# Up projection of a decoder layer: seven products for four pairs in every chunk but the first, and low parts made by DMA

## The chip, the cores and the metric

The kernel runs on one core of a Trainium2 chip. The metric is device time in microseconds (us), the median of several runs. The profile comes from one execution taken by the hardware profiler.

## The reference

One decoder layer on 256 tokens of width 2048 in float32: a normalised input projection, two kinds of attention, an output projection with a residual, and a feed-forward part. The change touches the feed-forward part and the step ahead of it:

```
x = x + rmsnorm(mixed @ w_out, norm_attn_post)
h = rmsnorm(x, norm_mlp_pre)                 # (256, 2048)
u = square(relu(h @ w_up))                   # w_up   (2048, 8192)
x = x + rmsnorm(u @ w_down, norm_mlp_post)   # w_down (8192, 2048)
```

## The kernel before, in words

**Matmuls in three passes.** Each float32 operand is split into two fp32r parts: `hi` is a copy rounded to fp32r (ScalarE, ACT) and `lo` is the rest, operand minus `hi` (VectorE, DVE). A product is three matmuls: hi by hi, hi by lo, lo by hi. `split` (L306, L307) does this; `split_gain` (L310, L311) multiplies by a per-partition gain on the way, since the rows of `w_up` have to be multiplied by `norm_mlp_pre`, which lies in `gcol`.

**Weights.** `Weights` keeps one plan of all weight tiles in the order in which TensorE (PE) uses them. A planned tile is loaded by SP (`load`, L190, five `raw` buffers) and split into one of eight pairs of `hi`/`lo` buffers. `get(i)` emits the loads and splits up to tile `i + 1 + ahead` (ahead is 6), as long as no more than eight tiles are unfreed, so tile `i` can be split when tile `i - 8` has been freed. Functions in `first` run when the plan reaches an entry, ahead of it. All engines work off their instructions in the order in which they were emitted.

**The up projection** goes in eight chunks `j` of 1024 columns of `w_up`. A chunk has 16 tiles `k` of 128 rows. A plain step `k` takes 12 matmuls of 128x128 by 128x512: two token blocks `b` times two halves `n` times three passes. Two neighbouring tiles can be taken together as a *pair* `kp` by seven products of 2x2 blocks instead of eight: 7 x 3 = 21 matmuls for what takes 24 as two plain steps. For this, `seven` loads both tiles (1 MB into `ab` or `ab2`), DVE forms sums `t`, `u` of their quarters (L361 to L366), and four tiles are split: the 512 wide `b11`, then `b`, `u`, `t`. On the left side `left_sums` forms sums of blocks of `hT` once, and multiplies by the gain while it does so. In the end `close` adds the shared sums to the four results. `UP_STEPS` gives the order: chunk 0 has no pairs, chunks 1 and 7 have three, chunks 2 to 6 four. In a chunk of four the order is the tiles 8, 9, 10, 11, pair 0, tile 12, pair 1, tile 13, pair 2, tile 14, pair 3, tile 15. "Tile 13" below is the plain tile of rows 13 of a chunk. The left sums of pairs 0 to 2 are made in chunk 0, those of pair 3 in chunk 1.

**Around it.** `residual` (one chain for each token block) normalises the output projection, adds it to `xs`, transposes `xs` on PE (`ht`) and splits the transposes, four channels `k` at a time, into `hT`; these instructions are interleaved with the first steps of chunk 0 by the estimated times of `Flow`. `up_evac` takes relu of an accumulator, transposes it on PE (`rt`), squares it and writes it to `uT[j]` (16 groups of 512 columns; for j 10 to 13 these lie in `ab` and `ab2`, so the last two chunks load some of their pairs as two `raw` tiles). In the down projection `split_u` splits one `uT` group ahead of its use, and the low parts are stored to HBM by SP (`ukeep`) and brought back by POOL.

Of the kernel before, what the change touches and what calls it, by code (L numbers as in the profile page):

```python
# [95 lines left out]
SUMS_AHEAD = 2  # L96


UP_PAIRS = [()] + [("ab", "ab2", "ab", "ab2")] * 5 + [("ab2", "ab", "raw", "ab"), ("ab", "raw", "raw")]


def up_steps(first, *groups):
# [3 lines left out]
    return steps  # L106


THREE = up_steps(range(6, 11), (11, 12), (13,), (14, 15))
FOUR = up_steps(range(8, 12), (12,), (13,), (14,), (15,))  # L110
UP_STEPS = [up_steps(range(16)), THREE] + [FOUR] * 5 + [THREE]

ST = 13 * 256
N_SEVEN = [sum(w == "w" for w, _ in steps) for steps in UP_STEPS]


DOWN_SEVEN = ((7, 11, 13, 17, 19, 23, 25, 29), range(3, 28, 2))
# [51 lines left out]
class Weights:  # L169


    def __init__(self, nc, pool, split, bufs, ahead):
        self.nc, self.pool, self.split_fn = nc, pool, split
        self.bufs, self.limit, self.ahead = bufs, bufs, ahead
        self.specs, self.tiles, self.done = [], [], []
        self.first, self.after = {}, {}

    def plan(self, *spec):

# [13 lines left out]
    def emit(self, upto):  # L193
        upto = min(upto, self.done.index(False) + self.limit, len(self.specs))
        while len(self.tiles) < upto:
            i = len(self.tiles)
            spec = self.specs[i]
            make = len(spec) == 1
            for f in self.first.pop(i, ()):
                f()  # L200
            if not make:
                src, nk, n, g = (*spec, None)[:4]
                w = nk * n
                raw = self.load(src if len(src.shape) == 3 else src.rearrange("(k p) n -> p k n", p=P), w, f"raw{i}")
                for f in self.after.pop(i, ()):
                    f()
            hi = self.pool.tile([P, CW], F32R, tag="hi", bufs=self.bufs, name=f"hi{i}")
            lo = self.pool.tile([P, CW], F32R, tag="lo", bufs=self.bufs, name=f"lo{i}")
            if make:
                spec[0](hi, lo)  # L210
                self.tiles.append((hi, lo))
                continue

            def v(t):
                return t[:, :w].rearrange("p (k n) -> p k n", k=nk)

            cuts = [(o, min(o + 512, w)) for o in range(0, w, 512)] if i < FINE else [(0, w)]
# [46 lines left out]
def layer(nc, tc, io):  # L264
# [49 lines left out]
    def tok(t, k, b):  # L314
        return t[:, k, b * P:(b + 1) * P]
# [25 lines left out]
    def up_weight(j, k):  # L341
        return io["w_up"][k * P:(k + 1) * P, j * CW:(j + 1) * CW]
# [33 lines left out]

    def seven_up(j, kp):
        def load():
            if UP_PAIRS[j][kp] == "raw":
                return [weights.load(up_weight(j, 2 * kp + i), CW, f"raw_w{j}_{kp}{i}") for i in range(2)]  # L380
            return load_two(late[UP_PAIRS[j][kp]], nc.gpsimd if (j, kp) > (1, 0) else nc.sync,
                            io["w_up"][2 * kp * P:(2 * kp + 2) * P, j * CW:(j + 1) * CW])

        return seven(load, lambda: [late["up"].tile([P, CW], F32, tag="T", bufs=2, name=f"{n}{j}_{kp}") for n in "tu"])

# [17 lines left out]
        st, left[c, kp] = down_parts(c, kp)  # L403
        nc.gpsimd.dma_start(out=st.bitcast(F32), in_=skeep[kp])

    def plan_seven(fetch_sums, fs, after, more=(), late_sums=0, last=()):

        at = max(len(weights.specs) - SUMS_AHEAD, after)
        fetch, sums = fetch_sums
        for n, f in (*more, (0, fetch), (-late_sums, sums), *((0, f) for f in last)):  # L410
# [6 lines left out]
    for j in range(FF // CW):  # L417
        wide_u.append([])
        for what, k in UP_STEPS[j]:
            if what == "k":  # L420

                ts = [weights.plan(up_weight(j, k), 1, CW, *([gcol[:, 8 + k:9 + k]] if j < 2 or k >= 2 * max(N_SEVEN) else []))]
            else:
                ts, after = plan_seven(*seven_up(j, k), after, (), SUMS_AHEAD + 1 if not k and N_SEVEN[j - 1] else 0)
            wide_u[j].append((what, k, ts))

    def down_weight(c, k):
# [432 lines left out]
    def residual(b):  # L860

        po, yg, hT = late["po"], late["yg"], late["hT"]
        nc.vector.reduce_sum(ssr[b][:, 0:1], ssy[b], axis=mybir.AxisListType.X)
        r = rstd_of(ssr[b][:, 0:1], 1, D, f"post{b}", (pws[:, 0, b:b + 1], pws[:, 1, b:b + 1]))

        def update(ns):
            cs = [slice(n * 512, (n + 1) * 512) for n in ns]
            for c in cs:
                nc.vector.scalar_tensor_tensor(out=xs[b][:, c], in0=yg[b][:, c], scalar=r, in1=xs[b][:, c],
                                               op0=OP.mult, op1=OP.add)  # L870
# [62 lines left out]
    def up_evac(j, b, i, acc, order):  # L933
# [6 lines left out]
        for k in range(4):  # L940
            transpose(t[:, k * P:(k + 1) * P], r[:, k * P:(k + 1) * P])
        if j not in uT:
            if j in (0, 1, 10, 11, 12, 13):
                t2 = late["u01" if j < 2 else "ab2" if j < 12 else "ab"][:, j % 2 * CW:(j % 2 + 1) * CW]
            else:
                tag = {"tag": "T", "bufs": 2} if j > 13 else {}
                t2 = late["up"].tile([P, CW], F32, name=f"uT{j}", **tag)
# [35 lines left out]
    def left_sums(kp):  # L983
# [6 lines left out]
        for i in range(2):  # L990
            nc.vector.tensor_scalar_mul(f[:, i * S:(i + 1) * S], f[:, i * S:(i + 1) * S], gcol[:, 8 + k + i:9 + k + i])
        fs, qs = [x.rearrange("p (k s) -> p k s", s=P) for x in (f, q)]
        keep = kp >= min(N_SEVEN[1:])
        n = 512 if keep else 384
        tt(out=qs[:, 0], in0=fs[:, 0], in1=fs[:, 1], op=OP.subtract)
        tt(out=qs[:, 3] if keep else fs[:, 1], in0=fs[:, 1], in1=fs[:, 3], op=OP.subtract)
        tt(out=qs[:, 1], in0=qs[:, 0], in1=fs[:, 3], op=OP.add)
        tt(out=qs[:, 2], in0=fs[:, 2], in1=qs[:, 1], op=OP.subtract)
        st = [late["st"][:, 768 * kp + i * n:768 * kp + (i + 1) * n] for i in range(2)]
        yield 3.0  # L1000
        for t, x in ((hs, f), (st, q[:, :n])):
            nc.scalar.activation(t[0], x, AF.Copy)
        yield 1.5
        for t, x in ((hs, f), (st, q[:, :n])):
# [46 lines left out]
    for j in range(FF // CW):  # L1051
# [9 lines left out]
        for t, b in order:  # L1061
# [247 lines left out]
```

## Time and profile before

| | |
|---|---|
| median of 3 runs | 1047.41 us (1047.2 to 1049.08) |
| profiled execution, from its first to its last instruction (span) | 1045.7 us |
| lies around the span, as the median less the span | 1.7 us |
| busy: PE, DVE, ACT, POOL | 99%, 80%, 60%, 5% of the span |
| HBM read, written | 212.72 MB, 15.73 MB |
| output projection's end to up projection's end | 354 to 702 us of the span |

A line of the timeline gives the start in us from the span's start, the duration in us, the engine, the line of the kernel, the operation, its output and inputs, their shapes, and in brackets the idle time of the engine ahead of it with what ended it. PE is TensorE's matmuls, PEld its weight loads. `q` behind an engine marks the DMAs that it issues. Matmuls overlap, so the row of one is longer than the time from one start to the next.

### The profile page before, as it was taken

Reading aid. Unit: us, or ns where it says so; the run is one execution under the profiler, and the core shown is the slowest. Engines: PE = TensorE matmul, PEld = TensorE weight load, DVE = VectorE, ACT = ScalarE, POOL = GpSimd, SP = SyncE. Lnnn points to the kernel's source line nnn. Section 1 sums busy time; section 2 is a strip of 40 time slices with the busy share of each in tenths; the row PEclk is TensorE's granted clock in tenths of the full one; section 3 lists DMA queues with packets and bytes.
Section 4 is the critical chain, followed back from the end, with each engine's and each line's share of the span. In section 5 each row is a group of like instructions: output and inputs, shape, how many; then the busy total and the mean of one; then the engine's idle time right before and its main releaser. Section 6 shows DMA issues by size and latency. Waiting matters only on the chain.

```text
span 1045.7 us, 13378 instructions
## 1 busy us (share of the span) xinstructions
PE 1035.7 (99%) x4837; PEld 863.2 (83%) x4837; DVE 838.7 (80%) x1122; ACT 630.4 (60%) x848; POOL 51.5 (5%) x83
## 2 busy tenths in 40 slices
PE   9999999999999999999999999999999999999996
PEld 6888889888888888888888888888888888888885
DVE  6676536567557669999999999897899978999995
ACT  6674436565545566665765667666567564766661
POOL 0000000000000000000000000000000000111100
PEclk9999999999999999999999999999999999999998
DMA  9975547454447295646657356378778767698952
GB/s 303 370 229 148 140 129 241 146 162 153 150 156 236 92 360 188 216 147 207 202 185 246 121 201 207 113 253 325 274 276 303 265 232 261 238 332 323 356 204 83
DMA packets 79938, 229.33 MB, mean 219 GB/s; under 512 B 6912, under 2 KB 11520, under 8 KB 79488
## 3 DMA queue, kind: packets, MB, share of 16 engines
q1 hardware_dynamic: 64576, 171.47, 48.9%
q0 software_dynamic: 14864, 56.63, 15.2%
q8 instruction: 38, 0.62, 0.3%
q10 hardware_dynamic: 432, 0.37, 0.1%
q14 instruction: 28, 0.23, 0.1%
HBM read 212.72 MB, written 15.73 MB: 218 GB/s over the span
## 4 chain that ended last, share of the span: by engine, by line
PE 97%; DVE 1%; issue 1%; ACT 0%; POOL 0%; DVEq 0%; POOLq 0%; ACTq 0%
PE y L296 25%; PE acc_u L296 24%; PE acc_o L296 8%; PE m L296 7%; PE md L296 5%; PE acc_qk L296 4%; PE acc_v L296 4%; PE acc_ckv L296 2%; PE acc_ukv L296 2%; PE acc_q L296 2%; PE acc_cq L296 2%; PE acc_k L296 2%; PE acc_uq L296 2%; PE rt L300 1%; PE sc_b L296 1%
## 5 line engine op out<-in xcount | busy, mean ns | idle before, releaser
L307 DVE TENSOR_TENSOR lo<-raw,hi 128x1024 fp32r<-128x1024 f32 (+3 forms) x213 | 241.5, 1152 | 89.8 <-ACT hi L306 89.1
L306 ACT ACTIVATE hi<-raw 128x1024 fp32r<-128x1024 f32 (+3 forms) x213 | 209.9, 999 | 73.6 <-PE y L296 16.1
L296 PE MATMUL y<-hi,uhi 128*128 128x512 f32 x370 | 144.4, 390 | 0.0
L296 PE MATMUL y<-hi,ulo 128*128 128x512 f32 x370 | 144.1, 389 | 0.0
L296 PE MATMUL y<-lo,uhi 128*128 128x512 f32 x370 | 144.0, 389 | 0.0
L296 PE MATMUL acc_u<-hi,hT_hi 128*128 128x512 f32 x356 | 141.7, 398 | 0.0
L296 PE MATMUL acc_u<-hi,hT_lo 128*128 128x512 f32 x356 | 139.2, 391 | 0.4 <-DVE hT_lo L307 0.4
L296 PE MATMUL acc_u<-lo,hT_hi 128*128 128x512 f32 x356 | 138.9, 390 | 0.0
L311 DVE SCALAR_TENSOR_TENSOR lo<-raw,gcol,hi 128x1024 fp32r<-128x1024 f32 x74 | 92.5, 1279 | 9.5 <-ACT hi L310 9.5
L310 ACT ACTIVATE hi<-raw,gcol 128x1024 fp32r<-128x1024 f32 x74 | 83.7, 1148 | 25.0 <-DMA raw<-in_w_up 11.7
L296 PEld LDWEIGHTS y<-hi,ulo 128*128 128x128 f32 x370 | 69.5, 188 | 14.4
L296 PEld LDWEIGHTS y<-lo,uhi 128*128 128x128 f32 x370 | 69.5, 188 | 14.3
L296 PEld LDWEIGHTS y<-hi,uhi 128*128 128x128 f32 x370 | 69.5, 188 | 14.2
L296 PEld LDWEIGHTS acc_u<-hi,hT_lo 128*128 128x128 f32 x356 | 66.8, 188 | 14.9 <-DVE hT_lo L307 0.8
L296 PEld LDWEIGHTS acc_u<-lo,hT_hi 128*128 128x128 f32 x356 | 67.0, 188 | 12.8
L296 PEld LDWEIGHTS acc_u<-hi,hT_hi 128*128 128x128 f32 x356 | 67.0, 188 | 12.8
L306 ACT ACTIVATE hi<-u 128x1024 fp32r<-128x1024 f32 (+1 forms) x38 | 37.4, 990 | 49.2 <-DVE u L366 35.4
L307 DVE TENSOR_TENSOR lo<-st_down,hi 128x1024 fp32r<-128x1024 f32 x42 | 50.4, 1220 | 3.0 <-ACT hi L306 2.8
L296 PE MATMUL acc_o<-hi,mixT_hi 128*128 128x512 f32 x128 | 51.8, 405 | 0.0
L306 ACT ACTIVATE hi<-st_down 128x1024 fp32r<-128x1024 f32 x42 | 43.9, 1052 | 12.6 <-PE y L296 9.5
L296 PE MATMUL acc_o<-hi,mixT_lo 128*128 128x512 f32 x128 | 50.2, 392 | 0.0
L296 PE MATMUL acc_o<-lo,mixT_hi 128*128 128x512 f32 x128 | 50.0, 391 | 0.0
(328 smaller groups left out, 2087.7 us busy)
## 6 DMA issues: line engine op xcount, KB each, us to landing
raw<-in_w_down SPq DMA_DIRECT2D x86, 512.0 KB, 5.8
raw<-in_w_up SPq DMA_DIRECT2D x76, 512.0 KB, 4.6
raw<-in_w_in SPq DMA_DIRECT2D x55, 512.0 KB, 4.9
ab<-in_w_up POOLq DMA_DIRECT2D x22, 1024.0 KB, 5.4
raw<-in_w_out SPq DMA_DIRECT2D x32, 512.0 KB, 4.2
ab_down<-in_w_down POOLq DMA_DIRECT2D x11, 1024.0 KB, 7.1
ukeep<-ulo SPq DMA_DIRECT2D x15, 512.0 KB, 7.0
ulo<-ukeep POOLq DMA_DIRECT2D x15, 512.0 KB, 6.2
```

Of the source, the lines that this page charges most:

```text
L296: nc.tensor.matmul(out, a, b, start=start, stop=stop)
L300: nc.tensor.transpose(out, a, ident)
L306: nc.scalar.activation(hi, src, AF.Copy)
L307: nc.vector.tensor_tensor(out=lo, in0=src, in1=hi.bitcast(F32), op=OP.subtract)
L310: nc.scalar.activation(hi, src, AF.Copy, scale=g)
L311: nc.vector.scalar_tensor_tensor(out=lo, in0=src, scalar=g, in1=hi.bitcast(F32), op0=OP.mult, op1=OP.subtract)
```

## The change

- Chunks 1 and 7 get a fourth pair, so every chunk but the first has four pairs and the order of the old chunks of four.
- For tiles 11, 13 and 15 of chunk 0, and 9, 10, 11, 13 and 14 of every other chunk (38 in all), `lo` is no longer made on DVE: ACT copies the weight to `hi`, ACT copies `hi` times -1 to `lo`, and a POOL DMA adds the weight from HBM to `lo`.
- The gain of tiles 8 to 15 moves from the weights into `hT`: in `residual` their splits are made one channel at a time, with a gain. Weight tiles keep a gain only in chunk 0, tiles 0 to 7.
- All pairs are loaded by SP into `ab` and `ab2` in turn, and the load stands four plan entries ahead of where it stood.
- The left sums of pair 3 follow those of pair 2 in chunk 0, and they too rewrite `hT`.
- `uT` 2 to 7 are stored to HBM by SP after their squares (`u_away`); groups 10 to 13 take the places of 4 to 7. Groups 2 and 3 come back in chunk 7, and 4 to 7 at the start of the down projection into `ab` and `ab2` (`u_back`).

```
-UP_PAIRS = [()] + [("ab", "ab2", "ab", "ab2")] * 5 + [("ab2", "ab", "raw", "ab"), ("ab", "raw", "raw")]
+N_SEVEN = [0] + [4] * 7
+K_SCALED = 8
+BY_DMA = {0: (11, 13, 15), **{j: (9, 10, 11, 13, 14) for j in range(1, 8)}}
...
-UP_STEPS = [up_steps(range(16)), THREE] + [FOUR] * 5 + [THREE]
+UP_STEPS = {0: up_steps(range(16)), 4: up_steps(range(8, 12), (12,), (13,), (14,), (15,)),
...
+UP_STEPS = [UP_STEPS[n] for n in N_SEVEN]
+PAIR_AHEAD = 4
...
+            if i in self.by_dma:
+                self.nc.scalar.activation(hi[:, :w], raw[:, :w], AF.Copy)
+                self.nc.scalar.activation(lo[:, :w], hi[:, :w].bitcast(F32), AF.Copy, scale=-1.0)
+                self.nc.gpsimd.dma_start(out=lo[:, :w], in_=src, accum_op=OP.add)
...
     def seven_up(j, kp):
         def load():
-            if UP_PAIRS[j][kp] == "raw":
-                return [weights.load(up_weight(j, 2 * kp + i), CW, f"raw_w{j}_{kp}{i}") for i in range(2)]
-            return load_two(late[UP_PAIRS[j][kp]], nc.gpsimd if (j, kp) > (1, 0) else nc.sync,
-                            io["w_up"][2 * kp * P:(2 * kp + 2) * P, j * CW:(j + 1) * CW])
+            buf = late[("ab", "ab2")[(sum(N_SEVEN[:j]) + kp) % 2]]
+            return load_two(buf, nc.sync, io["w_up"][2 * kp * P:(2 * kp + 2) * P, j * CW:(j + 1) * CW])
...
-                ts = [weights.plan(up_weight(j, k), 1, CW, *([gcol[:, 8 + k:9 + k]] if j < 2 or k >= 2 * max(N_SEVEN) else []))]
+                ts = [weights.plan(up_weight(j, k), 1, CW, *([gcol[:, 8 + k:9 + k]] if not j and k < K_SCALED else []))]
+                if k in BY_DMA[j]:
+                    weights.by_dma.add(ts[0])
...
-            split(hT[0][:, 4 * n:4 * n + 4, b * P:(b + 1) * P], hT[1][:, 4 * n:4 * n + 4, b * P:(b + 1) * P], tv)
+            for k in [range(4 * n, 4 * n + 4)] if 4 * n < K_SCALED else [range(k, k + 1) for k in range(4 * n, 4 * n + 4)]:
+                split(*[tok(x[:, k[0]:k[-1] + 1], slice(None), b) for x in hT], tv[:, k[0] - 4 * n:k[-1] + 1 - 4 * n],
+                      gcol[:, 8 + k[0]:9 + k[0]] if len(k) == 1 else None)
...
+        if b and 2 <= j < 8:
+            flow.start(u_away(j), 6.0)
+
+    U_HOME = {2: 8, 3: 9, 10: 4, 11: 5, 12: 6, 13: 7}
+    uaway = {}
+
+    def u_away(j):
+        uaway[j] = dram.tile([P, CW], F32, name=f"uaway{j}")
+        nc.sync.dma_start(out=uaway[j], in_=uT.pop(j).rearrange("p k s -> p (k s)"))
+        yield 0
+
+    def u_back(j, t):
+        nc.sync.dma_start(out=t, in_=uaway[j])
+        uT[j] = t.rearrange("p (k s) -> p k s", k=4)
...
-        yield from left_sums(2)
+        for kp in range(2, 4):
+            yield from left_sums(kp)
...
-            if (j, what, k, b) == (1, "k", 8, 0):
-                fourth = flow.start(left_sums(3), 20.0)
-            if j == 2 and t == 0:
-                flow.finish(fourth)
+            if (j, t, b) == (FF // CW - 1, 6, 0):
+                for i in (2, 3):
+                    u_back(i, late["up"].tile([P, CW], F32, tag=f"k{i}", bufs=1, name=f"uT{i}_back"))
...
+    for i in range(4, 8):
+        u_back(i, late["ab" if i < 6 else "ab2"][:, i % 2 * CW:(i % 2 + 1) * CW])
```

More of the change, by code (lines that the diff above doesn't have):

```diff
@@ L106, in up_steps @@
     return steps
-THREE = up_steps(range(6, 11), (11, 12), (13,), (14, 15))
-FOUR = up_steps(range(8, 12), (12,), (13,), (14,), (15,))
-UP_STEPS = [up_steps(range(16)), THREE] + [FOUR] * 5 + [THREE]
-ST = 13 * 256
-N_SEVEN = [sum(w == "w" for w, _ in steps) for steps in UP_STEPS]
+UP_STEPS = {0: up_steps(range(16)), 4: up_steps(range(8, 12), (12,), (13,), (14,), (15,)),
+            5: up_steps(range(10, 14), (), (14,), (), (), (15,))}
+UP_STEPS = [UP_STEPS[n] for n in N_SEVEN]
+PAIR_AHEAD = 4
+ST = 12 * 256
 DOWN_SEVEN = ((7, 11, 13, 17, 19, 23, 25, 29), range(3, 28, 2))
@@ L175, in __init__ @@
         self.specs, self.tiles, self.done = [], [], []
-        self.first, self.after = {}, {}
+        self.first, self.after, self.by_dma = {}, {}, set()
     def plan(self, *spec):
@@ L404, in down_back, with plan_seven @@
         nc.gpsimd.dma_start(out=st.bitcast(F32), in_=skeep[kp])
-    def plan_seven(fetch_sums, fs, after, more=(), late_sums=0, last=()):
+    def plan_seven(fetch_sums, fs, after, more=(), late_sums=0, last=(), ahead=0):
         at = max(len(weights.specs) - SUMS_AHEAD, after)
         fetch, sums = fetch_sums
-        for n, f in (*more, (0, fetch), (-late_sums, sums), *((0, f) for f in last)):
+        for n, f in (*more, (ahead, fetch), (-late_sums, sums), *((0, f) for f in last)):
             weights.first.setdefault(at - n, []).append(f)
@@ L420, in layer @@
             if what == "k":
-                ts = [weights.plan(up_weight(j, k), 1, CW, *([gcol[:, 8 + k:9 + k]] if j < 2 or k >= 2 * max(N_SEVEN) else []))]
-            else:
-                ts, after = plan_seven(*seven_up(j, k), after, (), SUMS_AHEAD + 1 if not k and N_SEVEN[j - 1] else 0)
+                ts = [weights.plan(up_weight(j, k), 1, CW, *([gcol[:, 8 + k:9 + k]] if not j and k < K_SCALED else []))]
+                if k in BY_DMA[j]:
+                    weights.by_dma.add(ts[0])
+            else:
+                ts, after = plan_seven(*seven_up(j, k), after, (), SUMS_AHEAD + 1 if not k and N_SEVEN[j - 1] else 0,
+                                       ahead=PAIR_AHEAD)
             wide_u[j].append((what, k, ts))
@@ L989, in left_sums @@
         tt(out=f, in0=hs[0].bitcast(F32), in1=hs[1].bitcast(F32), op=OP.add)
-        for i in range(2):
-            nc.vector.tensor_scalar_mul(f[:, i * S:(i + 1) * S], f[:, i * S:(i + 1) * S], gcol[:, 8 + k + i:9 + k + i])
         fs, qs = [x.rearrange("p (k s) -> p k s", s=P) for x in (f, q)]
-        keep = kp >= min(N_SEVEN[1:])
+        keep = k >= K_SCALED
         n = 512 if keep else 384
+        if not keep:
+            for i in range(2):
+                nc.vector.tensor_scalar_mul(f[:, i * S:(i + 1) * S], f[:, i * S:(i + 1) * S], gcol[:, 8 + k + i:9 + k + i])
         tt(out=qs[:, 0], in0=fs[:, 0], in1=fs[:, 1], op=OP.subtract)
@@ L998, in left_sums @@
         tt(out=qs[:, 2], in0=fs[:, 2], in1=qs[:, 1], op=OP.subtract)
-        st = [late["st"][:, 768 * kp + i * n:768 * kp + (i + 1) * n] for i in range(2)]
+        home = late["st4"] if keep else late["st"][:, 768 * kp:768 * kp + 768]
+        st = [home[:, i * n:(i + 1) * n] for i in range(2)]
+        split_of = ((st, q[:, :n]),) if keep else ((hs, f), (st, q[:, :n]))
         yield 3.0
-        for t, x in ((hs, f), (st, q[:, :n])):
+        for t, x in split_of:
             nc.scalar.activation(t[0], x, AF.Copy)
         yield 1.5
-        for t, x in ((hs, f), (st, q[:, :n])):
+        for t, x in split_of:
             tt(out=t[1], in0=x, in1=t[0].bitcast(F32), op=OP.subtract)
```

11 lines of the change are left out of this document (7 added, 4 removed).

## The prediction

> **What bounds the kernel now.** I read the page first, then the order of TensorE's instructions, then the stages.
>
> ```profile
> span 1045.7 us, 13378 instructions
> PE 1035.7 (99%) x4837; PEld 863.2 (83%) x4837; DVE 838.7 (80%) x1122; ACT 630.4 (60%) x848; POOL 51.5 (5%) x83
> PEclk9999999999999999999999999999999999999998
> PE 97%; DVE 1%; issue 1%; ACT 0%; POOL 0%; DVEq 0%; POOLq 0%; ACTq 0%
> ```
>
> TensorE (PE) is busy for 99% of the span at a full granted clock, and 97% of the chain that ended last is its own work. A busy matmul can still hide a gap, because the rows overlap: one row lasts 0.39 us while the next starts earlier. So I took the starts in order of time. One pair by seven products, of chunk 3:
>
> ```profile
> 500.14 0.39 PE L296 MATMUL m<-hi,hT_hi 128*128 128x512 f32 x1
> ...
> 504.69 0.39 PE L296 MATMUL m<-hi,hT_lo 128*128 128x512 f32 x1
> 504.92 0.39 PE L296 MATMUL acc_u<-hi,hT_hi 128*128 128x512 f32 x1
> ```
>
> From the first to the last line lie the pair's 21 matmuls; the next step starts at 504.92. (504.92 - 500.14) / 21 = 0.2276 us from start to start. That is the price of one matmul, not the 0.39 us of the row. Then the stages, by windows (busy us and count of PE, PEld, DVE, ACT, POOL; clock; DMA share; GB/s):
>
> ```profile
> 365.00:403.00 38.00, 37.59 (x172) 30.87 (x171) 29.50 (x45) 23.51 (x32) 2.39 (x3) 1.00 0.81 305
> 534.80:577.50 42.70, 42.70 (x197) 35.37 (x196) 41.01 (x45) 28.08 (x33) 2.85 (x4) 1.00 0.61 198
> 706.00:760.00 54.00, 54.00 (x248) 44.73 (x247) 43.06 (x49) 31.98 (x37) 1.43 (x2) 1.00 0.81 296
> ```
>
> The second row is one chunk with four pairs. VectorE (DVE) works 41.01 of 42.70 us, yet PE has no gap. So relieving DVE gives nothing by itself: only fewer matmuls shorten this stage, and whatever makes PE wait lengthens it. The one place in the up projection where PE loses time is its start, below.
>
> **The matmuls removed.** Chunks 1 and 7 go from three pairs by seven to four. A pair by seven is 21 matmuls where two plain steps are 24, so 2 x 3 = 6 matmuls go: 6 x 0.2276 = 1.37 us, all on the path. No other matmul or transpose goes.
>
> **The splits in `residual`.** For channels 8 to 15 each split of four channels at once becomes four splits with a gain. For token block 0 these stand on DVE just ahead of block 1's normalisation:
>
> ```profile
> 357.71 0.68 DVE L307 TENSOR_TENSOR hT_lo<-ht,hT_hi 128x512 fp32r<-128x512 f32 x1
> ...
> 359.50 0.68 DVE L307 TENSOR_TENSOR hT_lo<-ht,hT_hi 128x512 fp32r<-128x512 f32 x1
> 360.10 1.28 DVE L311 SCALAR_TENSOR_TENSOR lo<-raw,gcol,hi 128x1024 fp32r<-128x1024 f32 x1
> 361.30 0.15 DVE L863 TENSOR_REDUCE ssr<-ssy 128x1 f32<-128x4 f32 x1
> 361.48 0.27 DVE L500 TENSOR_SCALAR t_post<-ssr,pws 128x1 f32<-128x1 f32 x1
> 362.43 0.75 DVE L869 SCALAR_TENSOR_TENSOR x<-yg,rstd_post,x 128x512 f32<-128x512 f32 x1 [0.67 <-POOL rstd_post L501]
> 363.01 0.39 PE L296 MATMUL acc_u<-hi,hT_lo 128*128 128x512 f32 x1
> 363.32 0.63 PE L300 MATMUL ht<-ident,x 128*128 128x128 f32 x4
> 366.67 0.50 PE L296 MATMUL acc_u<-hi,hT_lo 128*128 128x512 f32 x1 [0.41 <-DVE hT_lo L307]
> ```
>
> DVE has no gap up to the reduction at 361.30, which feeds POOL's power and the update at 362.43; the update is done at 363.18 and the transposes that read it start at 363.32, 0.31 us after the matmul ahead of them instead of 0.23. PE waits there already by 0.08 us, so a delay on DVE passes through. A 512-wide split holds DVE 360.10 - 359.50 = 0.60 us. The nearest rows to the new ones are these, 128 wide:
>
> ```profile
> 386.72 0.28 DVE L995 TENSOR_TENSOR c<-c 128x128 f32<-128x128 f32 x1
> 387.04 0.29 DVE L996 TENSOR_TENSOR c<-c 128x128 f32<-128x128 f32 x1
> 387.25 0.29 DVE L997 TENSOR_TENSOR c<-c 128x128 f32<-128x128 f32 x1
> 387.57 0.29 DVE L998 TENSOR_TENSOR c<-c 128x128 f32<-128x128 f32 x1
> ```
>
> They start 0.21 to 0.32 us apart. Four take 0.84 to 1.28 us, 0.24 to 0.68 more than one wide split; two groups, 0.5 to 1.4 us. I take the middle, 0.265 each: 2 x (1.06 - 0.60) = 0.92 us, all of it PE's, since the wait is there already. The lower end for this step is a small gain: if the wait of 0.41 us at 366.67 closes through another order, -0.4.
>
> The Trainium skill (Perfetto Trace Analysis, Optimizing Scalar/DVE Operations) speaks against this step: it gives DVE a fixed cost of about 125 ns for each instruction on PSUM and advises grouping. By that figure three more instructions in each of two groups would cost an estimated 0.75 us, which the rows above bracket.
>
> **38 low parts by DMAs.** Off DVE, onto ScalarE (ACT): a copy to hi, a copy of -hi to lo, then a POOL DMA that adds the weight to lo. In a chunk DVE loses five instructions like this one, and ACT gains five like the second:
>
> ```profile
> 550.43 1.28 DVE L311 SCALAR_TENSOR_TENSOR lo<-raw,gcol,hi 128x1024 fp32r<-128x1024 f32 x1
> 545.24 1.05 ACT L306 ACTIVATE hi<-t 128x1024 fp32r<-128x1024 f32 x1
> 546.19 1.15 ACT L310 ACTIVATE hi<-raw,gcol 128x1024 fp32r<-128x1024 f32 x1
> 552.63 1.15 ACT L310 ACTIVATE hi<-raw,gcol 128x1024 fp32r<-128x1024 f32 x1
> 555.33 0.39 PE L296 MATMUL acc_u<-lo,hT_hi 128*128 128x512 f32 x1
> 562.81 0.39 PE L296 MATMUL acc_u<-lo,hT_hi 128*128 128x512 f32 x1
> 545.95 0.71 POOL L374 DMA_DIRECT2D ab<-in_w_up  x1 [8.65 <-DVE lo L307]
> ```
>
> DVE falls by 5 x 1.28 to about 34.6 us of a chunk, ACT rises from 28.08 by 5 x 1.05 to about 33.3: neither becomes a bound. What counts is the distance from ACT to PE. Tile 13's hi starts on ACT at 546.19 (the block before it runs back to back, 545.24 + 0.95); its -hi would end at 546.19 + 0.95 + 1.05 = 548.19; PE's first use of its lo is at 555.33. The DMA has 7.14 us from issue to landing. Tile 14: 552.63 + 2.00 = 554.63 to 562.81, 8.18 us. The others have more: a tile can start when the one eight places back is free, so PE has the seven tiles between; for 9 and 10 these are 57 matmuls (13.0 us), for 11 66 (15.0 us), in chunk 0 84 (19.1 us), less 2.0 us for ACT.
>
> No accumulating DMA is in this trace. The nearest rows (KB each, median us from issue to landing):
>
> ```profile
> raw<-in_w_up SPq DMA_DIRECT2D x76, 512.0 KB, 4.6
> ab<-in_w_up POOLq DMA_DIRECT2D x22, 1024.0 KB, 5.4
> ab_down<-in_w_down POOLq DMA_DIRECT2D x11, 1024.0 KB, 7.1
> ukeep<-ulo SPq DMA_DIRECT2D x15, 512.0 KB, 7.0
> ulo<-ukeep POOLq DMA_DIRECT2D x15, 512.0 KB, 6.2
> u<-in_w_down POOLq DMA_DIRECT2D x6, 1024.0 KB, 8.4
> c<-in_w_down POOLq DMA_DIRECT2D x4, 1024.0 KB, 8.9
> ```
>
> It writes 512 KB and must read both the weight and what is in lo, so I bound it by 4.6 us (512 KB, quiet) and 8.9 us (1024 KB, busy). The stage gets busier: 198 GB/s x 42.7 us = 8.5 MB in a chunk now, plus five tiles (2.6 MB) and, in three chunks, two stored tiles (1.0 MB) is 11 to 12 MB, 260 to 285 GB/s, near the down projection's 296. I take 6.2 us, the 512 KB POOL load under that traffic: it lands 0.9 us ahead of tile 13's use. Cost 0, and the cover is thin.
>
> **Moved at no cost.** The pair loads go from POOL to SP, four plan entries earlier; an SP load of a pair waits until its buffer is read, and the weight loads behind it wait too. Released at 545.95 (now POOL's row), it holds tile 14's weight behind it, which ACT wants at 552.63: 6.7 us, more than the 4.6 of a weight load. POOL's accumulating DMAs wait for ACT, and behind them stand only further ones. The six stores wait on SP for the squares; the down projection runs such stores on SP (ukeep, x15) with PE busy 54.00 of 54.00 us. The tiles that come back at the start of the down projection are split one group ahead of their use, after three groups of 48 matmuls (32.8 us) at the earliest. The fourth pair's left sums move into chunk 0, where DVE works 29.50 of 38.00 us. Dropped gains save about 0.1 us on tiles that are not waited for.
>
> **Sum.** Against the profiled span: 1045.7 - 1.37 + 0.92 = 1045.25 us. The median of the runs, 1047.41, stands 1.7 us above the span; with the same difference, 1046.96, rounded to 1046.9. A difference under 0.2% (2.1 us) is about what a measurement of this kernel can't tell from no change, so this is no change.
>
> **Rivals.**
> - *The accumulating DMA lands too late* (slower). It decides at 7.14 us from issue to landing; from 8.18 on tile 14 adds to it. At 8.4 us, the 1024 KB row: 7 chunks x (1.26 + 0.22) = 10.4 us, 1057.3. At 8.9: 7 x (1.76 + 0.72) = 17.4 us, 1064.3. For it: 1 MB is read in all, and the stage comes near the traffic under which 1024 KB took 7.1 to 8.9. Against it: 1024 KB from POOL takes 5.4 in the up projection. Chance 0.30. The Trainium skill (Collectives: The Full Stack, The bandwidth ceiling) says that a reducing DMA reads two sources over one ring and so runs at half a copy's rate; no run here shows it yet, and by that rule the 1024 KB rows are the right ones.
> - *SP's order makes tile 14 late* (slower). If the pair's megabyte ahead of its weight takes the 8.4 us of a busy load, the weight lands no sooner than 545.95 + 8.4 = 554.35, lo's copy ends at 556.35 and the DMA has 6.46 us; at 7.1 us that is 0.64 x 7 = 4.5 us, 1051.4. Chance 0.11.
> - *The delay in `residual` does not reach PE* (lower). Then 1.37 us stay, and with the wait of 0.41 us closed as well 1047.41 - 1.78 = 1045.6, still inside 0.2%. For more than 2.1 us something would have to go that no row of PE shows. Chance of over 0.2% faster: 0.09.
>
> **The numbers.** Forecast with its neighbours inside 0.2%: 0.50; faster 0.09; slower 0.30 + 0.11 = 0.41. The range's low end is 1045.2, 0.4 under the lowest case. Its high end, 1062, takes in the first rival up to a landing of about 8.7 us and leaves out what lies beyond. The forecast's own range, by its bounds (0.5 to 1.4 us in `residual`, -0.4 if the wait closes), is 1045.6 to 1047.5.
>
> **What would show it.** Right: six matmuls fewer; PE's start-to-start time still 0.2276 us; DVE near 35 us in a chunk, ACT near 33; accumulating DMAs landing in under 7.1 us; PE's wait ahead of block 1's transposes near 1 us instead of 0.08. Wrong: idle time of PE put down to POOL's DMA into lo at the 13th or 14th tile of each chunk, a period of a chunk above 42.7 us, or SP waiting on a pair's buffer while ACT waits for a weight.

## The result, and the profile after

The changed kernel takes 1093.01 us (median of 4 runs, 1090.13 to 1096.96), the kernel before 1047.88 us beside it (4 runs, 1047.2 to 1049.08). The ratio is 1.0435, 95% interval 1.0411 to 1.0458: 45 us slower, where I forecast no change and let the range end at 1062.0.

The page of the changed kernel (busy, clock and chain rows as before):

```profile
span 1090.6 us, 13430 instructions
PE 1046.5 (96%) x4831; PEld 865.4 (79%) x4831; DVE 804.3 (74%) x1103; ACT 667.8 (61%) x902; POOL 70.0 (6%) x99
PEclk9999999999999899899999999999999999999999
PE 78%; DMA 9%; issue 5%; DVE 4%; ACT 2%; SPq 0%; POOL 0%; POOLq 0%; DVEq 0%; ACTq 0%
```

Six matmuls are gone (4837 to 4831), DVE is 34 us less busy and ACT 37 us more, as the change intends. But PE's own work, 97% of the chain before, is now 78%; DMAs, DVE and "issue" hold 18%. And there are slices in which the clock is below full. The waits of PE (total us, times, longest):

```profile
PE acc_u L305 <- DMA lo<-in_w_up: 27.9, 13, 3.5
PE ht L309 <- DVE x L879: 5.0, 1, 5.0
PE rt L309 <- ACT r L949: 0.9, 4, 0.2
```

All of it lies in the up projection: from its first matmul to its last it took 347.2 us before and takes 392.1 now, and the 335.8 us behind it are the same. Nearly the whole difference of the two spans, 1090.6 - 1045.7 = 44.9 us, can be laid out from the trace. The three rows give 33.8 us. Around each of the 14 long waits some 0.16 us more is lost (a matmul at 537.44 behind one at 535.91 starts 1.30 us late by the spacing of 0.2276, and its row says 1.14), 2.2 us. The clock record has four stretches at 0.5, of 6.83, 6.83, 3.41 and 3.41 us, 20.5 us in all. In the first two PE was still waiting, for 2.9 and 1.3 us, which the rows have counted; half of the 16.3 us left, 8.1 us, is lost. Less 1.37 us for the six matmuls: 42.7 us. The other 2.2 us are steps of PE that are 0.1 to 0.2 us too long, most of them right behind these waits.

**The residual's wait.** Rows of DVE, ACT, PEld and PE at the splits of block 0:

```profile
357.52 0.35 DVE L320 SCALAR_TENSOR_TENSOR hT_lo<-ht,gcol,hT_hi 128x128 fp32r<-128x128 f32 x1
357.90 0.37 ACT L319 ACTIVATE hT_hi<-ht,gcol 128x128 fp32r<-128x128 f32 x1 [1.73 <-DVE hT_lo L320]
358.30 0.35 DVE L320 SCALAR_TENSOR_TENSOR hT_lo<-ht,gcol,hT_hi 128x128 fp32r<-128x128 f32 x1 [0.43 <-ACT hT_hi L319]
358.68 0.37 ACT L319 ACTIVATE hT_hi<-ht,gcol 128x128 fp32r<-128x128 f32 x1 [0.42 <-DVE hT_lo L320]
359.08 0.35 DVE L320 SCALAR_TENSOR_TENSOR hT_lo<-ht,gcol,hT_hi 128x128 fp32r<-128x128 f32 x1 [0.43 <-ACT hT_hi L319]
358.74 0.19 PEld L305 LDWEIGHTS acc_u<-hi,hT_hi 128*128 128x128 f32 x1
366.70 0.15 DVE L873 TENSOR_REDUCE ssr<-ssy 128x1 f32<-128x4 f32 x1
368.73 1.09 PE L309 MATMUL ht<-ident,x 128*128 128x128 f32 x4 [5.04 <-DVE x L879]
```

A low part has to wait for its own high part. But the next channel's high part waits for the low part before it, whose result it doesn't need. Both use the PSUM tile `ht`. They have `hT_hi` in common, too, one reading and the other writing it; but PEld reads `hT_hi` at 358.74 while ACT writes another channel of it (358.68 to 359.05), and neither waits. That leaves `ht`. So the two engines take turns, and a channel costs 358.30 - 357.52 = 0.78 us. The reduction that starts at 361.30 before starts at 366.70 now.

**Tiles 13 and 14.** The rows that decide in chunk 3, of ACT, POOL, SP and PE:

```profile
528.09 1.06 ACT L221 ACTIVATE lo<-hi 128x1024 fp32r<-128x1024 f32 x1
529.45 0.87 POOL L222 DMA_DIRECT2D lo<-in_w_up  x1 [20.92 <-ACT lo L221]
537.44 0.50 PE L305 MATMUL acc_u<-lo,hT_hi 128*128 128x512 f32 x1 [1.14 <-DMA lo<-in_w_up]
526.50 0.38 SPq L383 DMA_DIRECT2D ab<-in_w_up  x1
526.93 0.47 SPq L971 DMA_DIRECT2D uaway<-uT  x1
527.44 0.43 SPq L192 DMA_DIRECT2D raw<-in_w_up  x1
536.30 1.06 ACT L220 ACTIVATE hi<-raw 128x1024 fp32r<-128x1024 f32 x1 [2.86 <-DMA raw<-in_w_up]
538.74 0.87 POOL L222 DMA_DIRECT2D lo<-in_w_up  x1 [8.42 <-ACT lo L221]
547.95 0.50 PE L305 MATMUL acc_u<-lo,hT_hi 128*128 128x512 f32 x1 [2.74 <-DMA lo<-in_w_up]
```

Tile 13's DMA has from 529.45 to PE's first wish for `lo`, some 1.14 us ahead of 537.44: 6.85 us. It takes 8.0. Tile 14 is late before its DMA is issued: its weight stands on SP behind a pair and a store, was issued at 527.44 and reached ACT at 536.30, 8.9 us later. Then the DMA takes 9.2 us. In the waits of PE by time, tile 14 has 17.3 us of the 27.9, tile 13 has 7.1, and tile 11 of chunk 0, whose high part the residual's splits held up on ACT, 3.4 (0.84 in experiment 1, where the splits are grouped). The median landings of the three kinds of load (KB each, us), and ACT's wait for weights:

```profile
raw<-in_w_up SPq DMA_DIRECT2D x72, 512.0 KB, 8.2
ab<-in_w_up SPq DMA_DIRECT2D x28, 1024.0 KB, 5.7
lo<-in_w_up POOLq DMA_DIRECT2D x38, 512.0 KB, 7.7
ACT hi L220 <- DMA raw<-in_w_up: 20.5, 10, 4.8
```

**The clock.** Windows right behind four waits (the last three columns are clock, DMA share, GB/s), with two of the waits:

```profile
369.50:372.50 3.00, 3.00 (x10) 2.31 (x9) 2.96 (x6) 0.60 (x1) 0.97 (x1) 0.50 0.00 0
450.00:453.00 3.00, 3.00 (x8) 2.31 (x7) 0.00 (x0) 0.00 (x0) 0.00 (x0) 0.50 1.07 369
596.00:599.00 3.00, 3.00 (x15) 2.47 (x14) 0.00 (x0) 0.64 (x1) 0.00 (x0) 1.00 1.05 422
643.00:645.00 2.00, 2.00 (x6) 1.51 (x6) 0.12 (x1) 1.21 (x2) 0.47 (x1) 0.50 1.02 418
595.53 0.50 PE L305 MATMUL acc_u<-lo,hT_hi 128*128 128x512 f32 x1 [2.91 <-DMA lo<-in_w_up]
641.03 0.50 PE L305 MATMUL acc_u<-lo,hT_hi 128*128 128x512 f32 x1 [2.06 <-DMA lo<-in_w_up]
```

PE is "busy" throughout in all four, but in the rows at 0.50 it gets through fewer matmuls. The wait of 2.06 us was followed by half a clock and the longer one of 2.91 us was not; the last section says why.

### The profile page after: what moved, and what is told of

Its sections match the earlier page's. It is cut to its first block, busy times and chain, and to the rows that moved or that the text cites. A ratio compares the mean times of both kernels' runs of the same rounds, so it can differ in the third digit from the quotient of the medians.

```text
span 1090.6 us, 13430 instructions
## 1 busy us (share of the span) xinstructions
PE 1046.5 (96%) x4831; PEld 865.4 (79%) x4831; DVE 804.3 (74%) x1103; ACT 667.8 (61%) x902; POOL 70.0 (6%) x99
## 4 chain that ended last, share of the span: by engine, by line
PE 78%; DMA 9%; issue 5%; DVE 4%; ACT 2%; SPq 0%; POOL 0%; POOLq 0%; DVEq 0%; ACTq 0%
PE y L305 24%; PE acc_u L305 12%; PE acc_o L305 8%; DMA lo<-in_w_up 7%; PE md L305 5%; PE acc_v L305 4%; PE acc_qk L305 4%; PE m L305 3%; PE acc_ckv L305 2%; PE acc_ukv L305 2%; PE acc_q L305 2%; PE acc_cq L305 2%; PE acc_k L305 2%; DMA raw<-in_w_up 2%; PE acc_uq L305 2%
## 5 line engine op out<-in xcount | busy, mean ns | idle before, releaser
L316 DVE TENSOR_TENSOR lo<-raw,hi 128x1024 fp32r<-128x1024 f32 (+3 forms) x237 | 270.5, 1159 | 106.7 <-ACT hi L315 105.4
L315 ACT ACTIVATE hi<-raw 128x1024 fp32r<-128x1024 f32 (+3 forms) x237 | 235.3, 1006 | 86.4 <-DMA raw<-in_w_in 18.5
L305 PE MATMUL acc_u<-lo,hT_hi 128*128 128x512 f32 x344 | 138.4, 402 | 28.1 <-DMA lo<-in_w_up 27.9
L305 PE MATMUL acc_u<-hi,hT_hi 128*128 128x512 f32 x344 | 139.4, 405 | 0.0
L305 PEld LDWEIGHTS acc_u<-hi,hT_lo 128*128 128x128 f32 x344 | 66.1, 192 | 13.8
L220 ACT ACTIVATE hi<-raw 128x1024 fp32r<-128x1024 f32 x38 | 40.0, 1053 | 42.9 <-DMA raw<-in_w_up 20.5
L1074 DVE TENSOR_TENSOR c<-m,c 128x512 f32<-128x512 f32 x28 | 18.7, 689 | 58.5 <-ACT c L1071 57.1
L316 DVE TENSOR_TENSOR lo<-ab,hi 128x512 fp32r<-128x512 f32 (+1 forms) x56 | 52.5, 954 | 11.4 <-ACT hi L315 11.4
L222 POOL DMA_DIRECT2D lo<-in_w_up x38 | 33.3, 878 | 309.6 <-ACT lo L221 269.5
```

The lines of the kernel that those rows point to most:

```text
L220: self.nc.scalar.activation(hi[:, :w], raw[:, :w], AF.Copy)
L222: self.nc.gpsimd.dma_start(out=lo[:, :w], in_=src, accum_op=OP.add)
L305: nc.tensor.matmul(out, a, b, start=start, stop=stop)
L315: nc.scalar.activation(hi, src, AF.Copy)
L316: nc.vector.tensor_tensor(out=lo, in0=src, in1=hi.bitcast(F32), op=OP.subtract)
L1074: tt(out=c[out], in0=x, in1=y, op=op)
```

## Experiments

**1. The residual's splits grouped.** For eight channels: first four high parts on ACT, then four low parts on DVE.

```
-for k in ...: split(one channel, gain)
+for k in ks: nc.scalar.activation(hT_hi[k], tv[k], AF.Copy, scale=gain[k])
+for k in ks: nc.vector.scalar_tensor_tensor(out=hT_lo[k], in0=tv[k], scalar=gain[k], in1=hT_hi[k], ...)
```

> The changed kernel, but in residual the four hi copies of a group come first and then the four lo parts, instead of hi, lo, hi, lo. Theory 1 (two engines that read one PSUM bank are put one after the other, so the eight single splits go back and forth between ACT and DVE at 0.78 us a channel and hold up block 1's normalisation): the 5.04 us wait ahead of block 1's transposes falls under 1.5 us, the half-clock stretch of 6.8 us behind it goes (3.4 us), and ACT reaches chunk 0's tile 11 earlier, so its 3.44 us wait shrinks: 1093 less 8 to 12 is 1081 to 1085. Rival (the small instructions themselves are slow, or block 1 waits for something else): the wait stays over 3 us and the time over 1089. The waits at tiles 13 and 14 of the later chunks stay in both.

1085.37 us (1083.24 to 1086.28), ratio 1.0352 [1.0336, 1.0367]: 7.6 us back, 0.4 less than the least that was expected. DVE's four low parts and PE's two waits:

```profile
358.86 1.12 DVE L898 SCALAR_TENSOR_TENSOR hT_lo<-ht,gcol,hT_hi 128x128 fp32r<-128x128 f32 x4
PE acc_u L305 <- DMA lo<-in_w_up: 24.7, 14, 4.1
PE ht L309 <- DVE x L879: 0.7, 1, 0.7
```

The next instruction on DVE starts at 359.89, so four take 1.03 us, 0.26 each. The wait falls from 5.04 to 0.70 us. Taking turns was the cost, not the number of instructions.

**2. The single splits alone, in the kernel before.**

```
-split(four channels at once)
+for k in ([four] if n < 2 else singles): split(one channel)
```

> The kernel before with one part of the change alone: in residual channels 8 to 15 are split one at a time, hi, lo, hi, lo (without the gain, which stays in the weights). Theory 1: the wait ahead of block 1's transposes grows from 0.08 to about 5 us, and a stretch at half clock follows (3.4 us lost), with at most 1 us more at tile 8 of chunk 0: 1053 to 1057. If the halved clock needs more than this wait, 1052.5 to 1053.5. Rival (the changed kernel's 5 us came from elsewhere): under 1050.

1053.59 us (1052.89 to 1054.11), ratio 1.0051 [1.0036, 1.0066]. The same wait appears without anything else of the change, and behind it 3.41 us at half a clock:

```profile
PE ht L300 <- DVE x L869: 4.6, 1, 4.6
```

**3. No accumulating DMAs**, on the grouped kernel; those 38 low parts are made on DVE again.

```
-BY_DMA = {0: (11, 13, 15), **{j: (9, 10, 11, 13, 14) for j in range(1, 8)}}
+BY_DMA = {j: () for j in range(8)}
```

> As the first, and all low parts on DVE again; four pairs in chunks 1 to 7, pair loads on SP, stores and returns of six groups stay. Theory 1 (the low parts by DMA make PE wait, nothing else in the up projection does): no wait of PE on lo, about 1047.4 - 1.4 + 0.5 = 1046 to 1048.5. Rival 2 (the added traffic and the longer SP queue make everything late): 6 of the 26 MB added and SP's order stay, so waits of a few us remain, over 1051.

1053.12 us (1052.01 to 1053.57), ratio 1.0045 [1.003, 1.006]: 32.3 us less than experiment 1. PE waits for no DMA, and there is no half clock. But the 1046 to 1048.5 expected are missed. The larger part of what is left is new, two waits for the relus at the ends of chunks 1 and 7:

```profile
PE rt L309 <- ACT r L956: 3.7, 2, 2.0
```

**4. A plain load in place of the accumulating one**, on the grouped kernel; `lo` then holds the weight and not the rest.

```
-nc.gpsimd.dma_start(out=lo, in_=src, accum_op=OP.add)
+nc.gpsimd.dma_start(out=lo, in_=src)
```

> As the first, but POOL's DMA into lo is a plain load of the same 512 KB instead of an accumulating one; what PE multiplies in these 38 low parts is then the weight, not its rest. If accumulating itself is what is slow (it reads both sides), landing falls from 7.7 to about 6 us and the waits at tiles 13 and 14 fall from 26 us to under 8: about 1060. If the queue and the traffic around it are what is slow, landing stays over 7 us and the time within 5 us of the first kernel's.

1069.87 us (1069.4 to 1071.68), ratio 1.0212 [1.0195, 1.0229]. This lies between the two times expected. So 15.5 of experiment 3's 32.3 us go with the adding, and 16.8 stay with a plain load:

```profile
lo<-in_w_up POOLq DMA_DIRECT2D x38, 512.0 KB, 5.4
PE acc_u L305 <- DMA lo<-in_w_up: 12.3, 6, 3.1
```

It lands 2.0 us sooner than the accumulating one (7.4 in experiment 1). Five of the six waits are at tile 14, whose weight is still late: ACT waits 12.5 us for such weights in the up projection.

**5. The pairs on POOL**, as before the change, on the grouped kernel.

```
-load_two(buf, nc.sync, ...)
+load_two(buf, nc.gpsimd if (j, kp) > (1, 0) else nc.sync, ...)
```

> As the first, but the pair loads go back to POOL's queue (all but the first), still four plan entries early. If tile 14 is late since its weight stands behind a pair's megabyte on SP (ACT waited 2.86 us for it in chunk 3), ACT's waits on weights in the up projection go and tile 14's wait falls from about 2.8 to under 1 us in each chunk: 1060 to 1072. If only the accumulating DMA's landing counts, the time stays within 4 us of the first kernel's, or gets worse where an accumulating DMA stands behind a pair load on POOL.

1077.34 us (1076.26 to 1079.36), ratio 1.028 [1.0265, 1.0296]. ACT's waits for weights fall from 22.5 to 3.4 us, and PE's on the DMAs from 24.7 to 13.8. But a pair now queues with the accumulating DMAs, and the 1060 to 1072 of the first theory are missed:

```profile
ab<-in_w_up POOLq DMA_DIRECT2D x27, 1024.0 KB, 10.0
PE rt L309 <- ACT r L956: 6.1, 5, 2.1
```

The pairs are late instead of the weights: ACT waits 21.5 us for them. On neither queue did all loads land in time.

**6. Only the tiles between pairs: 13 and 14 of chunks 1 to 7**, on the grouped kernel (`BY_DMA = {0: (), 1..7: (13, 14)}`).

> As those, with low parts by DMA for tiles 13 and 14 alone. Theory 1: nearly all the waits of the first kernel on lo in chunks 1 to 7 come back (about 23 us with the halved clock's share of 7, and the closing sums' waits of up to 4 us return): 1070 to 1084. Rival (9 to 11 load the queues and make 13 and 14 late): waits under half, 1053 to 1065.

1081.35 us (1080.3 to 1081.63), ratio 1.0315 [1.0299, 1.033]; 14 DMAs, landing in 8.5 us, make almost all the wait that 38 make:

```profile
PE acc_u L305 <- DMA lo<-in_w_up: 24.2, 12, 3.6
```

**7. Only the tiles ahead of the pairs: 9, 10 and 11** (`1..7: (9, 10, 11)`).

> Four hi copies first in residual, and low parts by DMA only for tiles 9, 10 and 11 of chunks 1 to 7. Theory 1 (a DMA made low part costs PE only where the tile is needed too soon after its hi; 9 to 11 have 13 to 15 us of PE's work between a free buffer and their use): no wait on lo, and DVE reaches the closing sums 3.8 us earlier than in the kernel without DMAs, so the waits of 1.75 and 1.99 us at the ends of chunks 1 and 7 go: 1046.5 to 1048.5. Rival (every accumulating DMA costs, by its traffic): waits of a few us on 9 to 11, over 1051.

1055.49 us (1054.47 to 1057.31), ratio 1.0072 [1.0057, 1.0087]. PE waits for none of the 21 DMAs, landing in 6.6 us. It misses the 1046.5 to 1048.5 expected, by a wait at all seven ends of chunks: 1.72 us at the end of chunk 1, 0.22 to 0.64 at the next five, 2.08 after chunk 7. Rows of ACT and PE at the end of chunk 1, and the same in the kernel before at the end of chunk 2:

```profile
PE rt L309 <- ACT r L956: 5.7, 7, 2.1
452.19 1.06 ACT L315 ACTIVATE hi<-u 128x1024 fp32r<-128x1024 f32 x1 [3.74 <-DVE u L375]
453.15 0.67 ACT L956 ACTIVATE r<-acc_u,rstd_pre 128x512 f32<-128x512 f32 x1
453.88 0.66 PE L309 MATMUL rt<-ident,r 128*128 128x128 f32 x4 [1.72 <-ACT r L956]
```

```profile
492.55 1.06 ACT L306 ACTIVATE hi<-u 128x1024 fp32r<-128x1024 f32 x1 [3.74 <-DVE u L366]
493.51 0.67 ACT L937 ACTIVATE r<-acc_u,rstd_pre 128x512 f32<-128x512 f32 x1
494.67 0.60 PE L300 MATMUL rt<-ident,r 128*128 128x128 f32 x4
```

The second relu of a chunk stands behind the next pair's copy `hi<-u`, for which ACT idles 3.74 us until DVE has formed `u`. That order is not new: the kernel before has it too, with the same 3.74 us, and its relu starts 1.16 us ahead of PE's transposes, without a wait. What is new is the time left. DVE's closing sums start 7.3 us ahead of these transposes in the kernel before (487.40), and here 5.1 us ahead of PE's wish for them (447.03 to 452.16). Why they start later is not shown.

**8. Tile 12 as well** (`1..7: (9, 10, 11, 12)`).

> As the kernel with tiles 9, 10, 11, with tile 12 too. Tile 12 stands between pairs as 13 does, but has 57 matmuls (13.0 us) between a free buffer and its use, where 13 and 14 have 45 (10.2 us). Theory 1 (distance decides): no wait or under 0.5 us a chunk, 1046.5 to 1050. Rival (any tile between two pairs is late, since its weight stands behind a pair's megabyte on SP): waits of 1 to 3 us a chunk, 1055 to 1070.

1061.26 us (1059.9 to 1063.33), ratio 1.0132 [1.0115, 1.0148], 5.8 us for seven DMAs more. Four of tile 12's seven uses wait, 4.7 us in all (2.02, 1.29, 1.17, 0.21). So tile 12 is late even with 57 matmuls to its use, by less than tile 14. The time is in the rival's range, but the rival's reason isn't in the rows. In the four chunks with a wait, the copies of tile 12 wait for no weight; they stand behind the chunk's relus on ACT:

```profile
546.13 1.09 ACT L220 ACTIVATE hi<-raw 128x1024 fp32r<-128x1024 f32 x1
548.61 0.87 POOL L222 DMA_DIRECT2D lo<-in_w_up  x1 [14.95 <-ACT lo L221]
```

PE wants this `lo` at 553.96, 5.35 us after the issue, and the median landing is 6.4.

**9. The pairs and nothing else.** No DMA adds; the gain of tiles 8 to 15 stays in the weights; the residual's split is four wide as before.

```
+BY_DMA = {j: () for j in range(8)}
-weights.plan(..., gain if not j and k < K_SCALED else [])
+weights.plan(..., gain if not j or k >= K_SCALED else [])
+split(four channels at once)
```

> The changed kernel without low parts by DMA and without the gain in residual (the gain of tiles 8 to 15 stays in the weights, four channels are split at once as before): what is left is the fourth pair in chunks 1 and 7, the pair loads on SP, and the six groups in HBM. Theory 1: no wait of PE on any DMA; six matmuls less (1.37 us) against the waits for relu at the ends of chunks 1 and 7 that came with the full DVE (1.75 and 1.99 us): 1047.9 to 1050.5. Rival (SP's order and the 6 MB more cost by themselves): PE waits on weights, over 1052.

1053.49 us (1052.37 to 1054.87), ratio 1.0056 [1.0044, 1.0069]. Not a gain, and in the rival's range. PE loses 1.8 us at the end of chunk 1, at the same place as in experiment 7, and 2.2 at the end of chunk 7:

```profile
PE rt L309 <- ACT r L947: 4.2, 3, 2.2
696.97 2.12 SPq L973 DMA_DIRECT2D ab<-uaway  x4
707.57 1.06 ACT L315 ACTIVATE hi<-raw 128x1024 fp32r<-128x1024 f32 x1 [5.61 <-DMA raw<-in_w_down]
```

After chunk 7 there is no next pair. There two copies of the down projection's weights stand ahead of the relu, and the first waits 5.61 us for its weight; in the kernel before such a wait is 1.9 us at most. SP has just issued the returns of four groups, 2 MB, and the next three of these weights stand behind them (from 699.18). That is the rival's cause, by the order of the rows; the returns were not tried elsewhere.

**10. The same with less lookahead in the last pair of a chunk** (`weights.ahead -= 3` instead of 1).

> As that kernel, but in the last pair of a chunk the plan runs three entries less ahead instead of one, so fewer splits of plain tiles stand ahead of the closing sums on DVE. Theory 1 (the waits for relu come from the five splits ahead of the closing sums): the waits of 1.75 and 1.99 us go, 1046.3 to 1047.5, the six matmuls' worth below the kernel before. Rival (with three entries ahead the next chunk's first tiles come late): waits on lo at tiles 8 and 9, over 1050.

1066.79 us (1064.85 to 1068.93), ratio 1.0183 [1.0169, 1.0197]. A miss, with a time in the rival's range: tiles were held back so long that one came late itself, not 8 or 9 but tile 12, by 0.97 us in each of five chunks and 2.08 in chunk 7, with 3.67 us more for the relu after it and 3.41 us at half a clock behind each of the last two. It says nothing for or against the place.

```profile
PE acc_u L305 <- DVE lo L320: 6.9, 6, 2.1
```

**11 and 12. The relus earlier in ACT's program, their transposes later in PE's**, in the kernels of 9 and of 7.

```
-up_evac(2 * j + n, b, at[b, n], accs[b, n], o + 0.6)
+up_evac(2 * j + n, b, at[b, n], accs[b, n], 0.5 * (o + 0.6), lag)   # lag ahead of the transposes
```

> This is the pairs without any DMA (no accumulating DMAs, the residual split four wide as before), with the relus of a chunk's four accumulators put earlier in ScalarE's program and their transposes later in TensorE's. Without the reordering that kernel took 1053.49 us; TensorE waited 4.2 us for `r` (1.8 at the end of chunk 1, 2.2 at the end of chunk 7), and there ScalarE's second relu stood behind the copy `hi<-u` of the next pair, for which it idled 3.74 us. Theory: this place in ScalarE's program is the whole loss beside the pairs' six matmuls, so the wait on `r` goes and the time is 1048.5 to 1050, with the fast end 1047.7 - 1.37 = 1046.3 if nothing else comes late. Rival: VectorE is simply full with four pairs and no DMA (847 us busy), the next tile or sum is late instead, and it stays over 1052.

> The accumulating DMAs only for tiles 9, 10 and 11 of chunks 1 to 7, residual grouped, and the same reordering of relus and transposes. Without the reordering this took 1055.49 us, with 5.7 us of TensorE's waits on `r` in seven chunks and none on an accumulating DMA. Theory: the seven waits are all the one place in ScalarE's program; they go, and the time is 1048.5 to 1050.5 (residual wait 0.7 us left). Rival: ScalarE, with 42 copies more, delays something else by as much, and it stays over 1053.

1055.84 us (1054.53 to 1057.57), ratio 1.0077 [1.0063, 1.0091], and 1055.12 us (1052.97 to 1057.08), ratio 1.0072 [1.0059, 1.0084]. Both expectations are missed, and both times lie in the rival's range. The waits at the ends of chunks 1 to 6 go in both, though the edit moves relus and transposes at once, so it doesn't tell which of the two was needed. The wait after chunk 7 stays, longer than before (2.36 and 3.36 us), with 3.41 us at half a clock behind it. In experiment 12 ACT's row there is

```profile
710.50 1.06 ACT L315 ACTIVATE hi<-raw 128x1024 fp32r<-128x1024 f32 x1 [6.04 <-DMA raw<-in_w_down]
```

with a second such copy after it: after chunk 7 the relus stand behind the down projection's weights. In experiment 11 DVE's closing sums are now late by 0.23 us in most chunks, as its rival had it.

**13 and 14. The same place mended after chunk 7 as well:** there the lookahead is raised again 3 us later, so that one copy instead of two stands ahead of the relus. Number 13 has the DMAs for tiles 9, 10 and 11; number 14 has none, and early relus in chunks 1 and 7 only.

```
-weights.ahead = W_AHEAD
+flow.start(ahead_again(), 3.0)      # sets weights.ahead = W_AHEAD
```

> The kernel with accumulating DMAs for tiles 9, 10 and 11 and early relus (1055.12 us; TensorE waited 3.36 us for `r` at 711, after chunk 7, and its clock was halved for 3.41 us behind it), with one more edit, at the end of chunk 7 alone: the four relus come before the next copies, and the lookahead of the weights is raised again 3 us later, so that one copy `hi<-raw` of the down projection and not two stand in ScalarE's program ahead of the relus. Theory: the wait there falls to under 1.2 us (the second copy's wait on its DMA and its time were 2.74 us), the halving goes, and the time is 1050 to 1052. Rival: the wait stays over 2 us, since the first copy waits for a DMA (710.5) as late as before, and the time stays over 1054.

> The pairs without any DMA (1053.49 us; TensorE waits for `r` 1.8 us at the end of chunk 1 and 2.2 us at the end of chunk 7), with the relus early at the ends of chunk 1 and chunk 7 only and the lookahead raised 3 us later after chunk 7. Theory: both waits fall to under 0.5 us and the time is 1048.5 to 1050.5, still not under the kernel before by what a measurement can tell. Rival: over 1052, as the same edit in all chunks gave 1055.84 us.

1051.84 us (1050.59 to 1052.56), ratio 1.0033 [1.0021, 1.0046], and 1050.9 us (1050.39 to 1052.11), ratio 1.0029 [1.0019, 1.004]. In 13 the wait after chunk 7 falls to 0.6 us and the half clock goes, as expected. In 14, 0.4 us above the range expected, both mended waits go, but one of 1.72 us appears at the end of chunk 2, which had none. Of all fourteen, these two come nearest to the kernel before, and both are slower than it.

```profile
PE rt L309 <- ACT r L947: 1.7, 1, 1.7
```

## Why the prediction was wrong, step by step

The medians share out the 45.1 us: the residual's splits 7.6 (the change against experiment 1), the DMAs 32.3 (1 against 3), and 5.2 for what is left, four pairs with DVE making all low parts (3 against the kernel before).

- **The matmuls removed: right.** Six fewer, 0.2276 us each at a full clock. Beside them PE's trace has only the wait of 0.41 us to give back in this stretch, so some 1.8 us was the most there was to gain. No run's total shows it.
- **The splits in `residual`: the term was mis-sized,** 0.92 us against a wait of 5.04. Its price for a DVE instruction was right: 0.265 us was taken, 0.26 measured once they are grouped. What failed is that I counted DVE's instructions by themselves. As `split` emits them, DVE and ACT work on one PSUM tile in turn, at 0.78 us a channel, in two groups of four channels. The Trainium skill (PSUM — Partial Sum Buffer, PSUM bank collisions raise a hardware error) says that accesses of two engines to the same bank have to be kept apart, reads among them, and that a scheduler orders any two such instructions. The rows at 357.52 to 359.08 agree with that, and I weighed another page at this step, on the cost of one instruction. That taking turns is the cost, experiment 1 shows; that the turns come of the PSUM tile in common is what the rows leave, and the instructions were not tried on two banks.
- **38 low parts by DMAs: the rule that I put beside the row was nearer than the row.** I took 6.2 us for landing and allowed 7.14 us; in chunk 3 it took 8.0 and had 6.85. The first rival, 0.30, is what happened. Its price was too low: it took 8.4 us for both tiles, 10.4 us in all, while tile 14 took 9.2 us and was issued late, so the waits came to 27.9. The rule of half a copy's rate, which the Trainium skill (Collectives: The Full Stack, The bandwidth ceiling) gives for the reducing step of a collective, has the right sign here: 7.4 us against 5.4 for a plain load of the same size from the same queue. The ratio is 1.4, not 2, by medians of runs whose other traffic is not the same.
- **Moved at no cost: wrong for the pairs on SP.** The step set 6.7 us against a landing of 4.6 for tile 14's weight. With pairs, stores and weights on one queue the median landing is 8.2, and 8.9 for the tile shown. The queue alone doesn't make it so: in experiment 3, with the same loads on SP and no accumulating DMAs, it is 6.4. This is the second rival, counted as an alternative to the first; they happened together, and each made the other worse. Experiment 4 takes away the adding and experiment 5 the pairs from SP, and in each about half of PE's 24.7 us of waits on these DMAs stays (12.3 and 13.8). The step priced the groups that come back by their own use alone; that SP's weights for the down projection stand behind them (experiment 9) was in no term.
- **The clock was in no term.** I priced a late tile by its wait alone. 8.1 of the 44.9 us are matmuls at half a clock behind waits.
- **DVE and ACT: right as sums; the conclusion is open.** The prediction had them near 35 and 33 us in a chunk. Measured in a chunk of four pairs (DVE the third figure, ACT the fourth):

```profile
577.50:624.70 47.20, 43.15 (x196) 34.77 (x195) 34.66 (x39) 31.70 (x38) 3.98 (x6) 1.00 0.79 246
```

  I wrote that relieving DVE gives nothing by itself. For chunks 2 to 6 that stands. Chunks 1 and 7 with four pairs and DVE making every low part lose about 4 us behind the relus, which the changed kernel, with its DMAs, doesn't (0.9). That this is the relief of DVE is not shown. In experiment 7 DVE makes 21 low parts fewer than in experiment 3, and the wait for the relus is longer, 5.7 us against 3.7. In the changed kernel PE also stands still for 1.4 to 3.5 us at tile 14 of every chunk, shortly ahead of the relus, which gives ACT and DVE the time as well.
- **The range** took in landings up to about 8.7 us and no second cost at the same time. Its sum of rivals was made as if one at most could come true.

What stays open is the last 3 to 4 us of experiments 13 and 14. Each mend moved a wait of 0.4 to 1.7 us to another place (DVE's closing sums, the end of chunk 2). Whether some order of the four engines keeps the 1.37 us was not found; no run shows it.

## What to carry to other kernels

Where PE has no gap, price an edit by the distance of each hand-over on its path (issue to use, with what is queued ahead), and let several short distances fail together. When one split of a PSUM tile becomes several, emit all of one engine's parts and then all of the other's. A wait of two or three microseconds on PE can cost more than itself, so look at the granted clock behind it.

## What the runs showed of the hardware

- **A wait of 2.06 us can halve the clock.** The four stretches at 0.5 begin at 365.84, 447.76, 498.96 and 642.32 us; the distances are 24, 15 and 42 times 3.4133 us. So the clock is judged on a fixed grid of 3.41 us; the stretches of every other run that has more than one fit such a grid as well. Laid on it, a wait of the changed kernel that had 2.06 us or more in one window of the grid (2.06, 2.15, 2.22 and 2.51 us) was followed by half a clock, and the waits that gave no window more than 1.93 us were not: the wait of 2.91 us ahead of 595.53 is cut by a grid line at 594.54. In other runs 1.93 us (experiment 6) and 1.92 us (experiment 10) were enough, and 1.86 us (experiment 5) was not, so the limit lies near 1.9 us. Two stretches last two windows: in both, PE was idle for part of the first. The Trainium skill (TensorE: Matmul & The Clock Gate, What's actually happening) has the free-running window of 3413 ns, and the grid agrees; it puts the halving after a whole idle window, and by these rows some 55 to 60% of one is enough.
- **An accumulating DMA of 512 KB** into SBUF landed in 6.4 to 8.5 us (medians of the runs, with 14 to 38 of them), a plain one from the same queue in 5.4.
- **Two engines splitting one PSUM tile in turn** cost 0.78 us for each 128x128 channel, where the two instructions last 0.35 and 0.37 us and DVE's grouped ones take 0.26 each.
